# RMSNorm on one core: single-row stores moved between the loads of the second and third tile, and one load of 23 rows in place of 16 and 7

## The chip, the cores and the metric

The kernel runs on one core of a Trainium2 chip. The metric is the device time of one execution in microseconds (us); the profile adds the span of the profiled execution, which is some 1.8 us shorter than the time. Runs carry a state: "fast" unless a single run is more than 1.5% above the fastest of its kernel.

## The reference

```python
x = randn(16, 1024, 512)   # float32, 33.55 MB
gamma = ones(512)
rms = np.sqrt(np.mean(x ** 2, axis=-1, keepdims=True) + 1e-5)
return (x / rms * gamma).astype(np.float32)
```

Each of the 16,384 rows of 512 numbers is read once and written once, 67.11 MB in all.

## The kernel before

The rows are cut into four tiles of 128 partitions by 32 rows, numbered 0 to 3 in the code (so the second tile is tile 1). Three slots in on-chip memory hold tiles; tile 3 reuses slot 0. "Row" below means one such row across all 128 partitions, 256 KB (262,144 bytes). Each tile is worked on in groups of at most 16 rows: ScalarE (ACT) squares, VectorE (DVE) sums, both make the inverse root mean square; then GpSimd (POOL) scales a share of the rows and multiplies it by gamma, while ScalarE scales the others and VectorE multiplies them by gamma. All transfers are issued by SyncE (SP), in program order, into one queue served by 16 DMA engines.

```python
gamma_row = const.tile([1, D], fp32)
pieces = (0, 128, 224, 320, 416, D)

load(0, 0, 0, 8)                      # load(tile, slot, first row, end row)
for c0, c1 in zip(pieces, pieces[1:]):
    nc.sync.dma_start(out=gamma_row[:, c0:c1], in_=gamma.unsqueeze(0)[:, c0:c1])
load(0, 0, 8, 16)
load(0, 0, 16, 32)
load(1, 1, 0, 16)
load(1, 1, 16, 32)
# ... (cut)
def square_sums(ss, t, g, r, m, k):
    if m == 9:
        sq = slots[2][:, 23:32, :]    # rows 23..31 of slot 2 serve as scratch at first
    # ... (cut)
    nc.scalar.activation(out=sq[:, :m], in_=rows, func=AF.Square)
    nc.vector.tensor_reduce(
        out=ss[:, r : r + m, 0], in_=sq[:, :m], axis=mybir.AxisListType.X, op=OP.add
    )
# ... (cut)
def transfers(t, g):                  # called after group (t, g) is scaled
    if (t, g) == (0, 0):
        store(0, 0, 0, 1)
        load(2, 2, 0, 16)
        store(0, 0, 1, 2)
        load(2, 2, 16, 23)
    elif (t, g) == (0, 16):
        store(0, 0, 2, 3)
        load(2, 2, 23, 32)
        store(0, 0, 3, 16)
        store(0, 0, 16, 32)
        load(3, 0, 0, 16)
        load(3, 0, 16, 32)
    elif (t, g) == (1, 16):
        store(1, 1, 0, 32)
    elif (t, g) == (2, 16):
        store(2, 2, 0, 32)
    elif (t, g) == (3, 0):
        store(3, 0, 0, 16)
    elif (t, g) == (3, 16):
        store(3, 0, 16, 32)
```

## Time and profile before

| | before |
|---|---|
| time, median of the first 3 runs | 161.42 us (161.32 to 161.83) |
| span of the profiled run | 159.6 us |
| VectorE, ScalarE, GpSimd busy | 112.0, 107.8, 106.4 us |
| last compute ends | 138.70 us |
| packet time per DMA engine (the sum of all packets' durations over 16) | 156.53 of the 156.62 us from 1.75 to 158.37 |

The first part of the page of the kernel before gives the busy time of each engine, its share of the span and its number of instructions:

```profile
PE 2.0 (1%) x2; PEld 0.5 (0%) x2; DVE 112.0 (70%) x39; ACT 107.8 (68%) x108; POOL 106.4 (67%) x24
```

A packet record is one piece of a transfer on one DMA engine, with start, duration and size.

### The profile page before, as it was taken

The numbers are of one execution on the slowest core, as the hardware profiler recorded it, in microseconds if no ns is written. First come the engines' busy times: TensorE is split into PE (matmuls) and PEld (weight loads), VectorE is DVE, ScalarE is ACT, GpSimd is POOL, SyncE is SP. The second block draws the span as 40 slices with busy tenths as digits, with TensorE's granted clock in tenths as the row PEclk, the third lists the DMA queues.
The fourth block names the chain that finished last, engine by engine and source line by source line (L and its number), as shares of the span: only waits on it lengthen the run. The fifth ranks groups of instructions, "written<-read, shape, count | busy, mean of one in ns | idle before, by whom it ended". The sixth has DMA issues, their size and how long they took to land.

```text
span 159.6 us, 275 instructions
## 1 busy us (share of the span) xinstructions
PE 2.0 (1%) x2; PEld 0.5 (0%) x2; DVE 112.0 (70%) x39; ACT 107.8 (68%) x108; POOL 106.4 (67%) x24
## 2 busy tenths in 40 slices
PE   0050000000000000000000000000000000000000
PEld 0010000000000000000000000000000000000000
DVE  0028097998898999999999999999999009700000
ACT  3072957967999998999899899989960990000000
POOL 1000942994999599999999999999999990000000
DMA  5999999999999999999999999996996997999995
GB/s 199 428 427 501 419 394 435 485 394 394 460 394 394 429 454 407 427 452 452 468 394 394 509 411 394 526 526 263 526 509 279 526 476 312 394 468 452 394 435 222
DMA packets 2747, 67.12 MB, mean 421 GB/s; under 512 B 313, under 2 KB 314, under 8 KB 698
## 3 DMA queue, kind: packets, MB, share of 16 engines
q1 hardware_dynamic: 2746, 67.11, 98.2%
q14 instruction: 1, 0.01, 0.0%
HBM read 33.56 MB, written 33.55 MB: 421 GB/s over the span
## 4 chain that ended last, share of the span: by engine, by line
DVE 59%; ACT 22%; DMA 4%; ACTq 0%; issue 0%
DVE ss L97 36%; DVE slot L122 23%; ACT slot L118 8%; ACT slot L96 7%; ACT sq_psum L96 6%; DMA slot<-in_x_dram 4%; DVE ss L103 1%; ACT ss L102 1%; ACTq L208 0%; ACT gamma_b L165 0%
## 5 line engine op out<-in xcount | busy, mean ns | idle before, releaser
L109 POOL TENSOR_TENSOR slot<-slot,ss 128x3584 f32<-128x3584 f32 (+2 forms) x9 | 46.9, 5214 | 23.7 <-DVE ss L103 23.7
L110 POOL TENSOR_TENSOR slot<-slot,gamma_b 128x3584 f32<-128x3584 f32 (+2 forms) x9 | 59.3, 6585 | 0.7
L97 DVE TENSOR_REDUCE ss<-sq_psum 128x7 f32<-128x3584 f32 (+1 forms) x13 | 42.2, 3246 | 13.2 <-ACT sq_psum L96 13.2
L118 ACT ACTIVATE slot<-slot,ss 128x512 f32<-128x512 f32 x75 | 47.2, 706 | 4.7 <-DVE ss L103 4.7
L122 DVE TENSOR_TENSOR slot<-slot,gamma_psum 128x4608 f32<-128x4608 f32 (+2 forms) x9 | 41.3, 4590 | 8.7 <-ACT slot L118 8.7
L96 ACT ACTIVATE sq_psum<-slot 128x3584 f32<-128x3584 f32 (+1 forms) x13 | 34.6, 2658 | 6.0 <-DMA slot<-in_x_dram 5.2
L97 DVE TENSOR_REDUCE ss<-slot 128x9 f32<-128x4608 f32 x3 | 14.9, 4953 | 4.4 <-ACT slot L96 4.2
L97 DVE TENSOR_REDUCE ss<-sq_sbuf 128x5 f32<-128x2560 f32 x5 | 14.0, 2802 | 0.0
L96 ACT ACTIVATE slot<-slot 128x4608 f32<-128x4608 f32 x3 | 12.1, 4032 | 0.0
L96 ACT ACTIVATE sq_sbuf<-slot 128x2560 f32<-128x2560 f32 x5 | 11.6, 2320 | 0.0
L102 ACT ACTIVATE ss<-ss,eps_t 128x16 f32<-128x16 f32 (+2 forms) x9 | 2.7, 304 | 11.9 <-DVE ss L97 11.9
L103 DVE RECIPROCAL ss<-ss 128x16 f32<-128x16 f32 (+2 forms) x9 | 2.1, 235 | 0.4 <-ACT ss L102 0.4
L66 PE MATMUL gamma_psum<-gamma_row,ones_col 1*128 1x512 f32 x2 | 2.0, 1121 | 8.7 <-DMA gamma_row<-in_gamma_dram 8.7
L72 ACT ACT_TABLE_LOAD x1 | 1.3, 1283 | 1.1 <-PEq L197 1.1
L165 ACT COPY gamma_b<-gamma_psum 128x512 f32<-128x512 f32 x1 | 0.6, 564 | 0.0
L66 PEld LDWEIGHTS gamma_psum<-gamma_row,ones_col 1*128 1x128 f32 x2 | 0.5, 304 | 8.7 <-issue 8.7
L64 POOL MEMSET ones_col<- 1x128 f32 x1 | 0.2, 194 | 0.3 <-POOLq L197 0.3
L197 POOL MEMSET const-float32-0.0<- 128x1 f32 x1 | 0.1, 98 | 0.2 <-issue 0.2
L72 ACT ACTIVATE table<-eps_t 128x1 f32<-128x1 f32 x1 | 0.2, 203 | 0.0
L197 POOL MEMSET const-bfloat16-1.0<- 128x1 bf16 x1 | 0.1, 101 | 0.0
L197 POOL MEMSET const-uint8-127<- 128x1 uint8 x1 | 0.1, 101 | 0.0
L197 POOL MEMSET const-float32-1.0<- 128x1 f32 x1 | 0.1, 98 | 0.0
(1 smaller groups left out, 0.1 us busy)
## 6 DMA issues: line engine op xcount, KB each, us to landing
slot<-in_x_dram SPq DMA_DIRECT2D x6, 4096.0 KB, 21.7
out_dram<-slot SPq DMA_DIRECT2D x3, 4096.0 KB, 21.9
slot<-in_x_dram SPq DMA_DIRECT2D x2, 2048.0 KB, 8.5
out_dram<-slot SPq DMA_DIRECT2D x1, 3328.0 KB, 21.7
slot<-in_x_dram SPq DMA_DIRECT2D x1, 2304.0 KB, 14.2
slot<-in_x_dram SPq DMA_DIRECT2D x1, 1792.0 KB
out_dram<-slot SPq DMA_DIRECT2D x3, 256.0 KB, 29.4
gamma_row<-in_gamma_dram SPq DMA_DIRECT2D x4, 0.4 KB
```

The lines of the kernel that those rows point to most:

```text
L66: nc.tensor.matmul(gamma_psum[:, 0], ones_col, gamma_row, start=True, stop=True)
L72: nc.scalar.activation(out=table, in_=eps_t, func=AF.Sqrt)
L96: nc.scalar.activation(out=sq[:, :m], in_=rows, func=AF.Square)
L97: nc.vector.tensor_reduce(out=ss[:, r : r + m, 0], in_=sq[:, :m], axis=mybir.AxisListType.X, op=OP.add)
L102: nc.scalar.activation(out=ss[:, :n, 0], in_=ss[:, :n, 0], func=AF.Sqrt, bias=eps_t, scale=1.0 / D)
L103: nc.vector.reciprocal(out=ss[:, :n, 0], in_=ss[:, :n, 0])
L109: nc.gpsimd.tensor_tensor(out=part, in0=part, in1=by_row, op=OP.mult)
L110: last = nc.gpsimd.tensor_tensor(out=part, in0=part, in1=gamma_b.to_broadcast([P, share, D]), op=OP.mult)
L118: nc.scalar.activation(out=x[:, g + r, :], in_=x[:, g + r, :], func=AF.Copy, scale=rstd[:, r])
L122: scaled = nc.vector.tensor_tensor(out=part, in0=part, in1=gamma_psum.to_broadcast([P, r1 - r0, D]), op=OP.mult)
L165: nc.scalar.copy(out=gamma_b[:, 0], in_=gamma_psum[:, 0])
L197: nc = _bacc.Bacc("TRN2", target_bir_lowering=False, num_devices=1)
```

## The change

The intent: start the first writes earlier by putting the three single-row stores between the loads, the first between the halves of the second tile, the second ahead of the third tile, the third within it (where it already stood: the same rows go ahead of it before and after); and load the third tile in two pieces instead of three. One more gamma piece keeps the number of transfers at 24.

```diff
-    pieces = (0, 128, 224, 320, 416, D)
+    pieces = (0, 128, 208, 288, 368, 448, D)
@@
     load(1, 1, 0, 16)
-    load(1, 1, 16, 32)
@@ def transfers(t, g):
             store(0, 0, 0, 1)
-            load(2, 2, 0, 16)
+            load(1, 1, 16, 32)
             store(0, 0, 1, 2)
-            load(2, 2, 16, 23)
+            load(2, 2, 0, 23)
```

## The prediction

> **What bounds the kernel now.** I first read the second part of the profile page, the span in 40 slices, with the two lines of totals under it, because this kernel reads and writes every byte once and computes little per byte.
>
> ```profile
> DVE  0028097998898999999999999999999009700000
> DMA  5999999999999999999999999996996997999995
> GB/s 199 428 427 501 419 394 435 485 394 394 460 394 394 429 454 407 427 452 452 468 394 394 509 411 394 526 526 263 526 509 279 526 476 312 394 468 452 394 435 222
> DMA packets 2747, 67.12 MB, mean 421 GB/s; under 512 B 313, under 2 KB 314, under 8 KB 698
> ```
>
> The DMA row is nearly full from the first slice to the last, while VectorE (DVE) is thin for the first 12 slices and idle for the last five. The three dips (slices 28, 31, 34) are not holes. A packet is booked whole in the slice where it starts, and from 100 us on the packets carry 65,536 B and take 2418 ns, so one round of 16 falls into a slice or beside it (526 against 263). I therefore went to the packet records in the trace. Rebuilt from their starts and durations, all 16 engines are busy from the first packet at 1.75 us to the end of the last at 158.37 us: 156.62 us, of which packets fill 156.53. The queue never runs dry.
>
> Next, the chain of work that ended last, by engine and, in order of time, its last entry; then the waits of the issuing queue (SyncE), and two stretches of the windows view (length, busy time and count of PE, PEld, DVE, ACT and POOL, then clock, DMA share and GB/s).
>
> ```profile
> DVE 59%; ACT 22%; DMA 4%; ACTq 0%; issue 0%
> ```
> ```profile
> 131.61 7.09 DVE slot L122
> ```
> ```profile
> SPq L208 <- DMA out_dram<-slot: 19.4, 3, 9.6
> ```
> ```profile
> 139.00:158.40 19.40, 0.00 (x0) 0.00 (x0) 0.00 (x0) 0.00 (x0) 0.00 (x0) 1.00 0.94 407
> 158.40:159.60 1.20, 0.00 (x0) 0.00 (x0) 0.00 (x0) 0.00 (x0) 0.00 (x0) 1.00 0.00 0
> ```
>
> The chain suggests a VectorE bound, but it is followed back from the last issue, and its shares stop at 85%: the missing part is the drain, which the line of waits shows as 19.4 us that the program stands at its end for its stores. Compute ends at 138.70 us; the last store goes out at 138.76 and lands at 158.4, though its 4 MB (4096 KB) need only 8 packets of 1213 ns per engine, 9.7 us. The other 10 us it stood behind the previous store. The 16 DMA engines are the bound, and compute has about 9 us to spare at the end.
>
> **What the Trainium skill says.** "DMA: Bandwidth & Descriptors", section "Where 436 GB/s comes from", gives 435.2 GB/s as the ceiling of the 16 ports. The trace agrees: 32,768 B in 1213 ns on 16 engines is 432 GB/s; 67.11 MB at that rate is 155.3 us. Its section "Why small descriptors are slow (HBM only)" puts a fixed cost on every packet; the trace shows 2048 B in 84 ns, where the big packets' 27.0 B/ns would take 76. Its section "Queues, rings and completion order" says that descriptors are consumed in ring order on each engine, so a transfer's place in the queue sets its start; here packets run in order of issue. "Perfetto Trace Analysis", section "DMA Instruction — HWDGE (DVE, Sync)", says that the profiled window of such an issue covers descriptor generation and not data movement; the store issued at 138.76 shows 0.33 us and lands 20 us later, so 0.4 us issues say nothing of cost.
>
> **The change part by part.** The instruction order of PE, VectorE, ScalarE (ACT) and GpSimd (POOL) is identical by the comparison of the two builds; only SyncE's list moves. It has 24 transfers before and after, since one gamma piece comes and one load of the third tile goes.
>
> ```profile
> 0.74 0.38 SPq L45 DMA_DIRECT2D slot<-in_x_dram  x1
> 1.18 1.68 SPq L57 DMA_DIRECT2D gamma_row<-in_gamma_dram  x5
> 2.90 5.78 SPq L45 DMA_DIRECT2D slot<-in_x_dram  x4
> 26.92 0.35 SPq L49 DMA_DIRECT2D out_dram<-slot  x1
> 27.31 0.43 SPq L45 DMA_DIRECT2D slot<-in_x_dram  x1
> 27.84 0.38 SPq L49 DMA_DIRECT2D out_dram<-slot  x1
> 28.26 0.44 SPq L45 DMA_DIRECT2D slot<-in_x_dram  x1
> 28.80 0.43 SPq L49 DMA_DIRECT2D out_dram<-slot  x1
> 49.40 0.33 SPq L45 DMA_DIRECT2D slot<-in_x_dram  x1
> ```
>
> (1) *The second tile's upper half (rows 16 to 31) leaves the early group and is issued after the first single-row store*, which waits for VectorE's product at 26.89. So its issue moves from about 8 us to 27.3. What is queued then? Tile 0 and half of tile 1, whose last packets end near 31.5 us (landed 32.16). An issue takes 1.0 us to its first packet (0.74 to 1.75). Margin: 31.5 − 27.3 − 1.0 = 3.2 us. No hole, cost 0.
>
> (2) *Bytes are the same*, so moving the three stores costs nothing by itself: each is 128 packets of 84 ns on 16 engines, 0.67 us, wherever it stands. Now they run at about 31.5, 41.8 and 56.4 us instead of 41.4, 51.9 and 56.8.
>
> (3) *23 rows in one load instead of 16 and 7.* Before: 8 x 1213 + 8 x 535 = 13,984 ns per engine. After: 8 packets of 47,104 B; at the 27.1 B/ns of the largest packets that is 1738 each, 13,904. Gain 0.08 us.
>
> (4) *Six gamma pieces instead of five*: one more packet of 22 ns plus its 9 ns completion, on one engine: 0.03 us. Pieces landed 0.19 us apart (7.79 to 8.55), so the matmul at 8.69 starts some 0.2 us later; its product is first read at 15.20. Cost 0. The next load is issued 0.34 us later (1.68/5), at 3.24, while the first 2 MB keep the engines until 7.2. Cost 0.
>
> (5) *Completion semaphores rotate over eight*, as the waits in the build show. With six gamma pieces the ninth transfer, tile 0's upper half, now reuses that of the first load, and waits until 7.86 to be issued. Its predecessor keeps the engines until 12.0. Margin 12.0 − 7.9 − 1.0 = 3.1 us. From the first store on, every transfer has the same semaphore as before.
>
> (6) *Later arrivals.* Tile 1's upper half shifts by one store (0.67) from 42.24 to 42.9. Tile 2's rows 0 to 22 land together near 57.2, where rows 0 to 15 had landed at 52.57. Their first readers on ScalarE:
>
> ```profile
> 50.01 3.14 ACT L96 ACTIVATE sq_psum<-slot 128x3584 f32<-128x3584 f32 x1
> 63.96 3.14 ACT L96 ACTIVATE sq_psum<-slot 128x3584 f32<-128x3584 f32 x1
> ```
>
> Margins 7.1 and 6.8 us. Cost 0.
>
> (7) *What is not exact: the switch from loads to stores.* Packets just ahead of the first single-row store are stretched: the round at 38.64 averages 1512 ns and the next 1262 instead of 1213, together 0.35 us. Before the second store it is 0.10, the third 0.00, the fourth 0.05. The number of switches stays the same, but their places change; I allow +0.05 with an error of 0.25.
>
> Sum on the only resource that counts: −0.08 + 0.03 + 0.05 = 0.00 us. Predicted 161.4 us.
>
> **The rivals.** *A, the queue runs dry near 31 us*: if the store's wait on VectorE grew by more than 3.2 us, the engines would stand idle and every microsecond would go straight to the end: 162 to 164 us. Against it: the instructions ahead of that store (first load, squares, sum, scaling) keep their inputs and order. *B, compute starves*: if the 23-row load came 7 us late, VectorE would slip. Even so the end would stand: the third store goes out near 111 us and begins moving at 119.2, the last is issued 10 us before its turn. Compute may slip some 7 us before the queue feels it: still 161.4. *C, earlier stores help*: writing rows 10 us sooner would pay if it filled idle engines, or let a slot be reloaded sooner. Against it: there are no idle engines, and the reload of slot 0 waits for the 13-row store that landed at 71.4, behind the same bytes as now. Worth at most the 0.5 us of stretched packets: 160.9. *D, switches get dearer*: two further switches at the first one's price would add about 0.6: 162.0.
>
> **Range and chances.** Three runs of the kernel before spread by 0.5 us (161.32 to 161.83). C bounds the gain near 160.9 and D the loss near 162.0; I take 160.9 to 162.0. Over 2% faster means below 158.2, which is under the DMA floor: 155.3 of bytes, 1.75 to the first packet, 1.2 after the last, and 1.7 between profiled span (159.6) and measured time (161.33) give about 160.0. Chance 0.01. Over 2% slower needs a hole of 3.2 us, that is rival A at full size: 0.02. Within 2%: 0.97.
>
> **What would show it.** Right: the span within 0.5 us of 159.6; a full DMA row; the first single-row store issued at 26.9 and the load behind it at 27.3; ScalarE's squares starting at 50.0 and 64.0 as before; VectorE ending near 138.7 and the end still 20 us later; 47,104 B packets near 1740 ns. Wrong: a gap in the packets near 31 us (A); a new ScalarE wait on a load near 50 or 64 us (step 6); stretched packets adding up to over 1 us (D); or a span under 158.5, which would mean that the engines had been less busy than I read.

## The result

Four runs of the changed kernel took 161.39 to 161.47 us, median 161.43; four of the kernel before had a median of 161.38. The ratio is 0.9997, with a 95% interval of 0.9979 to 1.0015: the same. A ratio is the mean time of one kernel's fast runs over that of the other's of the same rounds, so it is not quite the ratio of the medians. On two later occasions the changed kernel had 161.52 beside 161.51 and 161.65 beside 161.70. All outputs are right.

The page of the changed kernel, its DMA row in 40 slices of the span and its packet totals:

```profile
DMA  6999999999989889999999999996996996999994
...
DMA packets 2605, 67.12 MB, mean 420 GB/s; under 512 B 299, under 2 KB 300, under 8 KB 684
```

The row is as full as before, and the bytes are the same; 142 packets fewer move them at the same mean rate. From the packet records, the packets of one engine take 156.67 us on average between 1.75 and 158.52, against 156.53 before.

The order of issue did change. The timeline of SyncE in the changed kernel (start, duration, line, what is issued, how many):

```profile
3.25 5.58 SPq L45 DMA_DIRECT2D slot<-in_x_dram  x3
27.05 0.35 SPq L49 DMA_DIRECT2D out_dram<-slot  x1
27.45 0.43 SPq L45 DMA_DIRECT2D slot<-in_x_dram  x1
27.98 0.38 SPq L49 DMA_DIRECT2D out_dram<-slot  x1
28.40 0.46 SPq L45 DMA_DIRECT2D slot<-in_x_dram  x1
28.95 0.44 SPq L49 DMA_DIRECT2D out_dram<-slot  x1
49.54 0.33 SPq L45 DMA_DIRECT2D slot<-in_x_dram  x1
```

Three loads instead of four go out early. The load at 27.45 is now the second tile's upper half, and the one at 28.40 the 23 rows. By the packet records its packets of 47,104 B took 1740 ns each. Two of the three writes of single rows now lie earlier in the queue: the first landed at 33.15 us instead of 42.87, the second at 43.48 instead of 53.28. The third has the same rows ahead of it as before and hardly moved (58.03 against 58.20).

Did a later load stall compute? The timeline of ScalarE in the changed kernel, at its first squares on the second tile's upper half and on the third tile:

```profile
50.14 3.14 ACT L95 ACTIVATE sq_psum<-slot 128x3584 f32<-128x3584 f32 x1
...
64.10 3.14 ACT L95 ACTIVATE sq_psum<-slot 128x3584 f32<-128x3584 f32 x1
```

Both come 0.14 us later than before and show no idle time ahead of them (a wait would stand in brackets at the end of the line). The whole chain is 0.14 us later, because the first load landed at 8.00 instead of 7.86. The end of the chain in the changed kernel, then SyncE's last wait, then two windows (length; busy time and count of PE, PEld, DVE, ACT, POOL; clock, DMA share, GB/s):

```profile
131.75 7.09 DVE slot L121
```
```profile
SPq L207 <- DMA out_dram<-slot: 19.4, 3, 9.6
```
```profile
139.00:158.40 19.40, 0.00 (x0) 0.00 (x0) 0.00 (x0) 0.00 (x0) 0.00 (x0) 1.00 0.95 409
158.40:159.70 1.30, 0.00 (x0) 0.00 (x0) 0.00 (x0) 0.00 (x0) 0.00 (x0) 1.00 0.00 0
```

Compute ends at 138.84, and the core then only drains stores for 20 us, exactly as before.

### The profile page after: what moved, and what is told of

It reads as the page before. It is cut to its first block, busy times and chain, and to the rows that moved or that the text cites. A ratio compares the mean times of both kernels' runs of the same rounds, so it can differ in the third digit from the quotient of the medians.

```text
span 159.7 us, 275 instructions
## 1 busy us (share of the span) xinstructions
PE 2.0 (1%) x2; PEld 0.5 (0%) x2; DVE 112.0 (70%) x39; ACT 107.8 (68%) x108; POOL 106.4 (67%) x24
## 4 chain that ended last, share of the span: by engine, by line
DVE 59%; ACT 22%; DMA 5%; ACTq 0%; issue 0%
DVE ss L96 36%; DVE slot L121 23%; ACT slot L117 8%; ACT slot L95 7%; ACT sq_psum L95 6%; DMA slot<-in_x_dram 5%; DVE ss L102 1%; ACT ss L101 1%; ACTq L207 0%; ACT gamma_b L164 0%
## 5 line engine op out<-in xcount | busy, mean ns | idle before, releaser
L95 ACT ACTIVATE slot<-slot 128x4608 f32<-128x4608 f32 x3 | 12.1, 4032 | 0.0
```

## The experiments

Twelve kernels were run, each derived from the changed kernel. Theory: the 16 DMA engines set the time, so a change of order costs nothing unless the queue runs dry. Rival: the chain through VectorE sets it. The kernel before ran beside them: medians 161.44 (e1 to e8), 161.51 (e9 to e11) and 161.70 (e12). Some of its runs are strays near 163.4 to 164.1 (see e12); where they were fast they pull the ratios, so I quote medians and ranges first. e1 to e8 ran on one chip, e9 to e11 on a second, e12 on a third, so each is best compared with what ran beside it.

### e1 and e2: make VectorE slower on purpose

```diff
-        nc.vector.tensor_reduce(
-            out=ss[:, r : r + m, 0], in_=sq[:, :m], axis=mybir.AxisListType.X, op=OP.add
-        )
+        again = 1 if (t, g, k) == (3, 16, 0) else 0      # e2: 3
+        for _ in range(1 + again):
+            nc.vector.tensor_reduce(
+                out=ss[:, r : r + m, 0], in_=sq[:, :m], axis=mybir.AxisListType.X, op=OP.add
+            )
```

> The changed kernel with one 128x7-row sum on VectorE done twice in the last group (3.83 us more on VectorE's chain, same result). If the 16 DMA engines are the bound, the last store is issued near 142.7 us instead of 138.9, still before its turn at about 148.3, and the time stays 161.4 (within 0.3). If VectorE's chain sets the end, as the chain view's 59% suggests, the time becomes 165.2.

> The same sum done four times, 11.5 us more on VectorE. If the DMA engines are the bound with some 9 us of slack, the last store is issued near 150.5 and reaches its first packet 1.0 us later, about 3 us after the previous store has left the engines: 164.5 (164 to 165.5), with a hole in the packets of that size. If VectorE sets the end: 172.9.

e1 took 161.34 us (161.24 to 161.43), e2 164.61 (164.43 to 164.72). The issue of the last store in e1, in e2 and in the unaltered changed kernel, each from the timeline:

```profile
142.87 0.33 SPq L49 DMA_DIRECT2D out_dram<-slot  x1
```
```profile
151.03 0.33 SPq L49 DMA_DIRECT2D out_dram<-slot  x1
```
```profile
138.90 0.33 SPq L49 DMA_DIRECT2D out_dram<-slot  x1
```

In e1 the last store goes out 4.0 us later and nothing comes of it. In e2 it goes out 12.1 us later and the time rises by 3.2. So compute had 12.1 − 3.2 = 8.9 us to spare at its end. The missing 3.2 us are a hole, in a window of e2 in which VectorE still multiplies by gamma and the DMA engines have almost nothing left. (The share of 0.33 is nearly all the last store's first packets, which start from 151.86 on and are booked whole. By the packet records fifteen engines end by 148.62 and one at 150.91.)

```profile
148.00:152.00 4.00, 0.00 (x0) 0.00 (x0) 2.96 (x1) 0.00 (x0) 0.00 (x0) 1.00 0.33 139
```

The rival, which wanted 165.2 and 172.9, falls: VectorE sets the end only when it starves the queue.

### e3 and e4: let the queue run dry ahead of the first store

```diff
-    load(1, 1, 0, 16)
+    load(1, 1, 0, 8)             # e4: no load here
@@ def transfers(t, g):
             store(0, 0, 0, 1)
+            load(1, 1, 8, 16)    # e4: load(1, 1, 0, 16)
             load(1, 1, 16, 32)
```

> Only 8 rows of tile 1 are queued ahead of the first single-row store instead of 16 (the other 8 follow the store as a load of their own). They leave the engines near 26.9 us, while the store, issued at 27.05, reaches its first packet near 28.05. DMA theory: a hole of about 1.2 us near 27 us that goes straight to the end: 162.6. If the store's place is free whatever the queue holds: 161.4.

> Nothing of tile 1 is queued ahead of the first single-row store; all its loads follow the store. Tile 0 leaves the engines near 22.1 us, the store's first packet comes near 28.05. DMA theory: a hole of about 6 us that goes straight to the end: 167.4. If VectorE's chain sets the end: tile 1's first half lands near 38.8 instead of 32.5 where ScalarE wants it at 37.4, so 1.4 us later: 162.8.

e3 took 163.85 us (163.75 to 163.93), e4 168.68 (168.42 to 168.90). A window of e3 around the expected hole, and one of e4:

```profile
26.80:28.10 1.30, 0.00 (x0) 0.00 (x0) 0.38 (x2) 1.30 (x1) 0.84 (x1) 1.00 0.11 43
```
```profile
22.00:28.00 6.00, 0.00 (x0) 0.00 (x0) 5.27 (x3) 3.43 (x3) 0.78 (x2) 1.00 0.00 0
```

The last column is GB/s: almost nothing for 1.3 us in e3, nothing at all for 6 us in e4, at the places worked out beforehand. By the packet records the holes are 1.26 and 6.13 us. That much is the theory, and it sets the place of a load that stands behind a computed store: enough must be queued ahead. But both kernels came out 1.25 us above the expectation. Against the changed kernel the engines are busy 0.78 us longer in e3 and 0.82 in e4, for the same bytes. The records show where: the first packets after the hole are stretched, by 0.60 us in all in both, as the first packets of every run are (0.47 to 0.62). So each of these two holes cost its own length and about 1.1 us more, of which 0.6 is starting again. I had not counted that. The rest is spread over later packets and over engines that end unevenly; in e3 the 9-row load alone is stretched by 0.62 us, against 0.24 in the changed kernel. In these three runs the start is dear only where loads follow the hole: after the hole in e2, which is longer than that of e3, a store follows, and its first two rounds are stretched by 0.04 us in all.

### e5 and e6: undo the gamma pieces; undo the 23-row load

```diff
# e5
-    pieces = (0, 128, 208, 288, 368, 448, D)
+    pieces = (0, 128, 224, 320, 416, D)
# e6
-            load(2, 2, 0, 23)
+            load(2, 2, 0, 16)
+            load(2, 2, 16, 23)
```

> The new order of loads and stores with the old five gamma pieces: the part that the sixth piece plays. It takes one small packet from one engine and moves the semaphores back by one place. DMA theory: 161.4, within 0.1 of the changed kernel. If the sixth piece is needed to keep the eight semaphores free for the reordered transfers, some issue waits and the time rises by over 0.5.

> The changed kernel with the third tile loaded in 16, 7 and 9 rows again, all else as changed. By packet sizes the split costs 0.08 us: 161.5, not to be told from 161.4. If the size of the load mattered for arrival (rows 0 to 15 land 4.6 us earlier), the time would fall by over 0.5.

e5 took 161.55 us in the median; four of its six runs lie at 161.39 to 161.65 and two are strays (163.28, 164.12). e6 took 161.68, with five runs at 161.46 to 162.55 and a stray at 163.79. Neither part is worth a measurable amount. e6 is inconclusive as to the 0.08 us that the split should cost: the run-to-run scatter is larger. The profiled run of e6 is the one at 162.55; see e12 for what made it long.

### e7 and e8: no single-row stores at all

```diff
     load(1, 1, 0, 16)
+    load(1, 1, 16, 32)           # e8: load(1, 1, 0, 32) for both, and five gamma pieces
@@ def transfers(t, g):
         if (t, g) == (0, 0):
-            store(0, 0, 0, 1)
-            load(1, 1, 16, 32)
-            store(0, 0, 1, 2)
             load(2, 2, 0, 23)
         elif (t, g) == (0, 16):
-            store(0, 0, 2, 3)
             load(2, 2, 23, 32)
-            store(0, 0, 3, 16)
+            store(0, 0, 0, 16)
             store(0, 0, 16, 32)
```

> The changed kernel without any single-row store: tile 1 and the third tile's first 23 rows are loaded straight on, and the first store writes 16 rows at once instead of 1, 1, 1 and 13. DMA theory: same bytes, the queue stays full; 384 packets of 84 ns (2.02 us per 16 engines) become part of 32768 B packets (1.81 us), -0.21, and the stretched packets ahead of three switches may fall away, up to -0.3: 160.9 to 161.3. If the early stores earn their keep by starting the writes 30 us sooner, leaving them out makes it slower by over 0.5.

> The previous kernel with tile 1 loaded in one transfer of 32 rows (65536 B packets at 2418 ns instead of pairs of 1213) and five gamma pieces. DMA theory: 0.06 us less for the packets and one semaphore write less, so 160.8 to 161.2; it should be the fastest of all by a few tenths, never by 2%. Tile 1 lands whole near 41.6, and ScalarE wants its first rows at 37.4: compute slips by about 4.3 us, which the slack of some 7 us covers. If compute sets the end, it is 165.7.

Both expectations fell. e7 took 162.05 us (161.82 to 162.46), 0.6 above the kernel before (161.44) and 0.4 to 0.5 above e5 and e6, all on the same chip; its ratio of 1.0021 hides that, since the kernel before had two strays in these rounds. e8, meant to be the fastest, took 163.46, in two clusters of three runs (162.88 to 162.98 and 163.94 to 164.33).

The queue in e7 never runs dry. What is longer are packets: those of the 9-row load of the third tile, the last load before the first store. The same stretch of 5.5 us within that load, in e7 and in the changed kernel (packets are booked whole where they start, so a share can pass 1):

```profile
55.30:60.80 5.50, 0.00 (x0) 0.00 (x0) 5.50 (x3) 5.14 (x7) 5.39 (x1) 1.00 0.98 349
```
```profile
57.30:62.80 5.50, 0.00 (x0) 0.00 (x0) 5.50 (x3) 5.14 (x8) 5.42 (x2) 1.00 1.05 432
```

The engines are as busy, but move 349 GB/s against 432. A packet of 18,432 B takes 686 ns undisturbed; in e7 the mean is 809 and the longest 1340, in the changed kernel 716 and 980. Eight packets per engine make that 0.98 us of stretch against 0.24. The three early stores therefore earn about half a microsecond by being there at all, whereas I had expected to gain at least 0.2 us from leaving them out. The stretch is the largest single difference in the packets, but it isn't the whole account: e7 also saves 0.2 us of small packets and 0.29 us of stretch ahead of the first single-row store, so that its packets take only 0.20 us more per engine in all (156.87 against 156.67), and the profiled run was 0.46 us longer (161.93 against 161.47). The remainder, at the end of the run, is not explained.

e8 adds a second lesson. Its tile 1 lands in one piece, so ScalarE's squares wait (the bracket), and with VectorE's sums the scratch rows in slot 2 come free late. ScalarE's first squares on tile 1 and the issue of the 9-row load, from two timelines of e8:

```profile
42.10 3.16 ACT L95 ACTIVATE sq_psum<-slot 128x3584 f32<-128x3584 f32 x1 [4.46 <-DMA slot<-in_x_dram]
```
```profile
54.24 0.33 SPq L45 DMA_DIRECT2D slot<-in_x_dram  x1
```

The load is issued at 54.24 instead of 49.54, and by the packet records its first packet starts at 55.18, as the queue runs out: the packets of its first round are stretched by 0.60 us, and the whole load by 1.77. The 7 us of slack that I wrote into the expectation held for the end of the kernel and not for this load, which waits for VectorE too.

### e9 and e10: which early store is it?

```diff
# e9: only the first is kept, where the change has it
-            store(0, 0, 1, 2)
-            store(0, 0, 2, 3)
-            store(0, 0, 3, 16)
+            store(0, 0, 1, 16)
# e10: tile 1 whole at first, and only one early store, ahead of load(2, 2, 23, 32)
             load(2, 2, 0, 23)
+            store(0, 0, 0, 1)
```

> The changed kernel with only the first of the three single-row stores (between the halves of tile 1); rows 1 to 15 follow in one store. Leaving all three out cost 0.6 us, of which the trace showed about 1.0 us of stretched packets in the 9-row load ahead of the first store. Theory P: one early switch from reading to writing is enough to make later ones cheap; then the 9-row load is stretched by 0.3 us or less and the time is 161.3 to 161.5. Theory Q: what helps is a small store right ahead of the 9-row load; then it is stretched by about 1.0 again and the time is 162.0.

> Only one single-row store, placed between the 23-row and the 9-row load of the third tile; both halves of tile 1 are loaded straight on. Theory P (the first switch is the dear one, wherever it comes): the 47104 B packets ahead of this store are stretched by 0.3 to 1.0 us and the 9-row load by little: 161.4 to 162.0. Theory Q (a small store right ahead of the 9-row load is what helps): the 9-row load is stretched by 0.3 or less: 161.3 to 161.5.

e9 took 161.70 us (161.59 to 161.88, no strays). e10 took 162.85 in the median, but in two clusters: three runs at 161.91 to 162.07 and three at 163.63 to 164.22. The stretch of the 9-row load, from the packet records: 0.98 us without an early store (e7), 0.50 with the first alone (e9), 0.59 with one just ahead of it (e10), and 0.24, 0.36 and 0.32 in three profiles of the changed kernel with all three. Neither P (one early switch is enough) nor Q (only the store right ahead of the load counts) is borne out. In these six profiles the stretch is smaller with more early stores, but that is no rule: e3, with all three, has 0.62 (behind its hole), and the kernel before, with three at other places, 0.05. The first long store also changes with their number (16, 15 or 13 rows), which was not tested apart. Nor does the stretch make e10 slower than e9: its packets take less time in all (156.71 against 156.83 us per engine), but one engine ended at 159.02 when the others had ended by 158.47. What in the hardware makes load packets longer ahead of a store stays open.

### e11 and e12: the changed kernel again, and the strays

> The changed kernel again, unaltered, on the chip of the last experiments and beside the same runs of the kernel before: 161.4 (161.35 to 161.5), with at most one or two of its runs near 163.4, as the kernel before showed 2 of 9 there. If the change made such stray runs rarer or more frequent, their share would differ clearly.

> The changed kernel once more, for one question alone: stray runs. So far 4 of 25 runs of the kernel before came out near 163.4 to 164.1 us, and none of 9 of the changed kernel. Chance reading: with the same share of 16% some 1 of these 6 is a stray, and 9 without one is no surprise (0.84 to the 9th is 0.21). Reading that the change removes them: again none here, while the kernel before shows one or two in the same rounds. The median is 161.4 to 161.6 either way.

e11 took 161.52 us (161.34 to 161.60); e12 took 161.65 (161.40 to 163.70), with two strays among six. Over all rounds the changed kernel had 2 strays in 15 runs, the kernel before 6 in 36: no sign that the change touches them. By luck the profiled run of e12 was one of the strays, at 163.70. A window of it, and the same one of the first profile of the changed kernel:

```profile
158.30:160.90 2.60, 0.00 (x0) 0.00 (x0) 0.00 (x0) 0.00 (x0) 0.00 (x0) 1.00 0.06 25
```
```profile
158.30:160.90 2.60, 0.00 (x0) 0.00 (x0) 0.00 (x0) 0.00 (x0) 0.00 (x0) 1.00 0.00 0
```

A DMA share of 0.06 is one engine of 16: one engine alone is still moving, two last packets of 32,768 B, from 158.34 to 160.77 us. By the landings of each transfer its engine was 0.86 us behind the median already when the first load landed, 2.17 at 64 us when the third tile was loaded, and 2.34 at the end. So in this run the slowest of 16 engines set the time, 2.3 us late. For the other strays that is only likely; none of them was profiled. But the profile of e6, a run at 162.55 that I did not count as a stray, shows the same in small: fifteen engines end by 158.48 us and one at 159.52. Why one engine was slower is open.

## Why the prediction was right

The prediction was right: 161.43 measured for 161.4 predicted, and for its own reason, since e1 to e4 show that the DMA queue is the bound. That the number fits to 0.03 us is in part luck: the terms as the packets show them are −0.06, +0.03 and +0.2, some +0.17 us where the sum had 0.00. The two profiled runs differ by 0.14 (161.47 against 161.33), the medians by 0.05; both are within the scatter of single runs. By its own steps:

- **The bound.** Shown by e1 and e2. I had put the slack of compute at the end at about 9 us; it is 8.9. The chain view's 59% for VectorE, read alone, would have misled. One small misreading: by the row shown, VectorE is thin only in slices 1 to 3 and 5, not in the first 12. Nothing rests on it.
- **Step 1, no hole near 31 us.** Right: no gap in the packets there. e3 and e4 show that the margin was real, and that behind it every microsecond of hole reaches the end, with about 1.1 us on top that rival A did not have, 0.6 of it for starting again.
- **Step 2, the place of the stores is free.** Right for these two orders. But "costs nothing by itself" is not the whole truth about such stores: that they exist at all is worth about half a microsecond (e7), which neither the step nor rival C saw.
- **Step 3, the 23-row load.** 8 x 1740 = 13,920 ns against 13,984: 0.06 us where I had 0.08. Too small for e6 to show.
- **Steps 4 and 5, gamma and semaphores.** The matmul began at 8.90 instead of 8.69, 0.2 us later as worked out; e5 shows the part to be worth nothing.
- **Step 6, later arrivals.** Tile 1's upper half landed at 42.82 (42.9 predicted), the 23 rows at 57.38 (57.2); ScalarE waited for neither.
- **Step 7, the stretched packets.** Allowed +0.05 us with an error of 0.25. Over all packets the stretch was 1.05 us before and 1.25 and 1.32 in two profiles of the changed kernel. The two rounds ahead of the first store fell from 0.35 to 0.29, those ahead of the second from 0.09 to nothing, and the 9-row load rose from 0.05 to 0.24 and 0.36. The first packets of the run, which the change does not touch, rose by another 0.1. The +0.2 fits within the error, and was the largest single term.
- **Rivals.** A describes what e3 and e4 then did, but for the cost on top, and B what e1 and e2 did. C gave nothing in this change. D's dearer switches were +0.1 to +0.2 us, not +0.6.

The skill's statement on ring order fits the traces before and after, in which the packets of the transfers started in the order of issue, and its ceiling of 435.2 GB/s agrees with the 432 GB/s within packets.

## What to carry to other kernels

When the DMA engines are busy from the first packet to the last, moving transfers about is worth little in itself (here 0.05 us, within the scatter); ask first whether something is queued at every moment, and take the margin from issue times and packet ends. Check the bound by slowing the engine that the chain view accuses a little: if the time does not move, as in e1, the view was wrong. And a few small stores strewn early among a long run of loads can pay, here about half a microsecond, even where no engine is idle, so do not tidy them away unmeasured.

## What the Trainium skill lacked or had wrong

- "DMA: Bandwidth & Descriptors" does not say that load packets ahead of a store in the same queue can get longer. Here packets of 18,432 B rose from 686 ns to a mean of 809 without early stores (0.98 us per engine), and to 716 in one profile of the changed kernel with three.
- The same page gives a fixed cost per transfer but none for starting after idleness. Here the first packets of each run, and the first loads after a hole, were stretched by about 0.5 to 0.6 us in all, the worst of 16,384 B from 611 ns to 1274 and more; a store after a hole (e2) was stretched by 0.04 us only.
- The same page's table in "Latency and other measured facts" calls engines 7 and 15 usually slower and guesses at a cause tied to descriptors that GpSimd makes. Here all transfers were issued by SyncE, and in one run one engine still ended 2.3 us behind the median; the packed trace does not number the engines, so which it was is not known.
- "Perfetto Trace Analysis", section "Identifying the Most-Contended Engine", advises HBM utilization for DMA. That pointed the right way here. Over the whole span (420 and 421 GB/s) it did not show the stretched packets; in a window of 5.5 us the rate did (349 GB/s against 432), at a busy share of 0.98, which bears out the page's distrust of occupancy. That it was the packets that got longer showed only in their durations by size, which the section does not mention.
